# An encoder's projection stage: eight single PSUM banks, paired peaks, later key turns and another bank layout in the attention loop

## The chip, the core and the metric

The kernel runs on one core of a Trainium2 chip. The metric is device time in microseconds (us) for one launch, the median of three runs. TensorE (PE) multiplies matrices and writes PSUM, which has eight banks of 512 float32 values on each of 128 partitions. VectorE (DVE), ScalarE (ACT) and GpSimd (POOL) do the rest of the arithmetic, and SyncE (SP) issues the transfers between HBM and the on-chip memory.

## The reference

An encoder of two layers runs over 1024 tokens of width 1024, all in float32. Layer 0 mixes tokens by grouped-query attention (16 query heads, 4 key and value heads, head size 64) with normalised and rotated queries and keys; layer 1 by centred means over windows. Each layer then attends to 256 memory tokens and ends with a gated feed-forward part with a width-3 convolution. The change lies in the attention of layer 0:

```python
qkv = h @ w_qkv                      # h = rmsnorm(x, gain)
q = rmsnorm(q, q_gain); k = rmsnorm(k, k_gain)
q = apply_axial_rope(q, cos, sin) * (HEAD_DIM ** -0.5)
k = apply_axial_rope(k, cos, sin)
scores = jnp.einsum('bkgqd,bksd->bkgqs', q_blk, kt)
p = jax.nn.softmax(scores, axis=-1)
```

## The kernel before, in words

The **projection stage** is the first 165 us. Tokens are cut into eight tiles of 128 (t = 0..7). A float32 product is made of three matmuls, high by high, low by high and high by low (L755, L756, L757; `mm3`), after ACT has cut the high part of an operand (L668 for weights, L686 for x with its gain) and DVE the low part (L671, L684). One output tile of 512 columns takes eight slices of the inner size, 24 matmuls. The list `QKV` holds eight K items (keys and values of tile t, 512 columns) and sixteen Q items (two halves of eight heads by eight tiles), with "S" items, the peaks, between them.

The first four K tiles are built together, slice by slice, in the order in which x and the weights arrive: `plan_start` issues gcol (the gain), then for each k a piece of x and a piece of the weights. Before them TensorE runs `WARM` transposes of the identity (L1249).

A K or Q tile then goes through `plan_head`. ACT writes its square into PSUM (L1039), DVE sums it per head (L1043, L1044), POOL raises it to the power -1/2 (L1048, `rstd`). DVE multiplies by the rotation tables, "crossed" into a buffer `rb` (L1065) and "straight" into `kr` or `qn` (L1071); POOL adds both (L1075); DVE (L1080) or ACT (L1083) scales. Then TensorE turns the result (transposes at L1123 for keys, L1157 for queries) into PSUM, from where ACT and DVE cut high and low halves (L668, L671). `plan_k` also makes `dk`, shifted keys, which are turned too.

The row factors of x come from `plan_rows`: a load, ACT's square of a tile of x with its sum (L954, its output thrown away into a PSUM tile of two banks) and two POOL operations (L955, L956).

**Peaks.** A visit of the peaks takes 128 queries of two heads and half of the keys: one matmul over 64 rows for each head (L801) gives 512 scores per query, and their maximum (L807) is kept in `nm` for the softmax. In this stage they go to a PSUM tile of 1024 columns (pA, two banks) and one reduction of 1024 columns takes both. `PEAKS` says after which Q item one visit stands: one each after items 3 to 14.

**What sets the order.** The program text adds steps to a planner (class `Plan`). Each step has a kind with a cost, what it needs, what it gives, and which buffers it takes; "late" is a due time. The planner simulates the engines and writes the steps of each engine in the order it finds. In `main`, the product of an item is added at once and the steps behind it ("after", with the turns) `LAG` + `kind_lag` items later.

**PSUM.** In this stage the pool "psq" holds pA (two banks) and six single banks pB. In the attention loop, pool "psl", it is pO (one bank), pS (three, peaks at L801) and pT (two tiles of two banks, scores at L1311); the banks are laid out in the order in which the names are first asked for, L1256 to L1262. The loop is a planner's order as well.

## Time and profile before

| | us |
|---|---|
| median of 3 runs | 2401.65 |
| the runs | 2404.88, 2401.65, 2400.08 |
| the profiled execution's own time | 2403.06 |
| its span | 2401.30 |
| TensorE busy | 2380.1 (99%) |
| DVE, ACT, POOL busy | 1858.5, 1199.8, 407.4 |

In the rows of a timeline stand the start, the length, the engine, the line, the operation, what it writes and reads, and how often; in brackets the idle time of the engine before it and what ended it. The rows of the chain of waits (the chain of work that ended last) have start, length and what it was. In the groups by line stand total busy time and the mean of one in ns, then the idle time before. Matmuls overlap, so the distance of two starts, not the length, tells what one costs. All lines are those of the kernel before.

### The profile page before, as it was taken

The numbers are of one execution on the slowest core, as the hardware profiler recorded it, in microseconds if no ns is written. First come the engines' busy times: TensorE is split into PE (matmuls) and PEld (weight loads), VectorE is DVE, ScalarE is ACT, GpSimd is POOL, SyncE is SP. The second block draws the span as 40 slices with busy tenths as digits, with TensorE's granted clock in tenths as the row PEclk, the third lists the DMA queues.
The fourth block names the chain that finished last, engine by engine and source line by source line (L and its number), as shares of the span: only waits on it lengthen the run. The fifth ranks groups of instructions, "written<-read, shape, count | busy, mean of one in ns | idle before, by whom it ended". The sixth has DMA issues, their size and how long they took to land.

```text
span 2401.3 us, 32595 instructions
## 1 busy us (share of the span) xinstructions
PE 2380.1 (99%) x11857; PEld 1901.6 (79%) x11857; DVE 1858.5 (77%) x2594; ACT 1199.8 (50%) x1982; POOL 407.4 (17%) x394
## 2 busy tenths in 40 slices
PE   9999999999999999999999999999999999999998
PEld 7764444688988888888888888798888888888887
DVE  6669998559763898888887768986389888888875
ACT  6545556435452555555454427555255555545442
POOL 5567777310110000000000012011000000000001
PEclk9999999999999999999999999999999999999999
DMA  7000001426951243334387623695124333448752
GB/s 255 1 1 15 15 19 50 159 75 215 320 173 62 75 121 99 110 88 117 116 293 230 200 88 124 223 330 192 65 71 128 92 110 88 120 122 278 251 189 101
DMA packets 323436, 322.93 MB, mean 134 GB/s; under 512 B 32612, under 2 KB 253132, under 8 KB 323276
## 3 DMA queue, kind: packets, MB, share of 16 engines
q1 hardware_dynamic: 323276, 320.85, 41.7%
q8 instruction: 93, 1.52, 0.3%
q14 instruction: 67, 0.55, 0.1%
HBM read 233.30 MB, written 82.64 MB: 132 GB/s over the span
## 4 chain that ended last, share of the span: by engine, by line
PE 88%; DVE 4%; DMA 3%; issue 3%; ACT 1%; POOL 1%; SPq 0%; POOLq 0%; DVEq 0%; ACTq 0%
PE pB L755 22%; PE pB L757 22%; PE pB L756 22%; PE pO L1353 4%; PE pT L1311 3%; PE pA L757 3%; PE pA L755 3%; PE pA L756 3%; PE pS L801 2%; DVE R L671 1%; PE pB L324 1%; DMA scr<-in_xt 1%; PE pS L1391 1%; DMA X<-in_ffn_w_down 1%; PE pA L2367 0%
## 5 line engine op out<-in xcount | busy, mean ns | idle before, releaser
L756 PE MATMUL pB<-R,R 128*128 128x512 f32 (+1 forms) x2732 | 1030.1, 377 | 0.2 <-DVE R L671 0.2
L755 PE MATMUL pB<-R,R 128*128 128x512 f32 (+1 forms) x2668 | 1011.1, 379 | 4.2 <-DVE scr L440 2.1
L757 PE MATMUL pB<-R,R 128*128 128x512 f32 (+1 forms) x2664 | 1004.0, 377 | 1.3 <-DVE R L671 1.2
L756 PEld LDWEIGHTS pB<-R,R 128*128 128x128 f32 x2732 | 514.9, 188 | 94.0 <-DVE R L671 1.5
L755 PEld LDWEIGHTS pB<-R,R 128*128 128x128 f32 x2668 | 502.8, 188 | 101.9 <-issue 4.8
L757 PEld LDWEIGHTS pB<-R,R 128*128 128x128 f32 x2664 | 501.8, 188 | 94.5 <-DVE R L671 3.1
L668 ACT ACTIVATE R<-scr 128x512 fp32r<-128x512 f32 (+3 forms) x376 | 269.1, 745 | 230.3 <-DMA scr<-Gs 60.3
L671 DVE TENSOR_TENSOR R<-scr,R 128x512 fp32r<-128x512 f32 (+2 forms) x340 | 289.3, 878 | 35.2 <-ACT R L668 34.8
L728 POOL TENSOR_SCALAR ms<-ss 128x1 f32<-128x1 f32 x52 | 14.7, 283 | 1626.6 <-ACT R L736 1281.1
L671 DVE TENSOR_TENSOR R<-X,R 128x512 fp32r<-128x512 f32 x258 | 175.4, 687 | 49.0 <-ACT R L668 48.6
L668 ACT ACTIVATE R<-X 128x512 fp32r<-128x512 f32 x258 | 160.8, 630 | 100.1 <-PE pB L756 50.3
L438 ACT COPY scr<-pB 128x512 f32<-128x512 f32 x156 | 91.0, 583 | 177.8 <-PE pB L757 170.6
L807 DVE TENSOR_REDUCE nm<-pS 128x1 f32<-128x512 f32 x232 | 148.3, 683 | 21.2 <-PE pS L801 20.0
L1318 ACT ACTIVATE X<-pT 128x1024 f32<-128x1024 f32 x128 | 124.7, 1023 | 73.5 <-PE pT L1311 71.4
L755 PE MATMUL pA<-R,R 128*128 128x512 f32 (+1 forms) x420 | 150.6, 359 | 0.0
L757 PE MATMUL pA<-R,R 128*128 128x512 f32 (+1 forms) x420 | 150.2, 358 | 0.1
L756 PE MATMUL pA<-R,R 128*128 128x512 f32 (+1 forms) x420 | 149.9, 357 | 0.0
L1353 PE MATMUL pO<-X,XV 128*64 128x512 f32 x512 | 124.1, 605 | 0.3 <-ACT X L1318 0.3
L2058 DVE TENSOR_TENSOR X<-pB,X 128x512 f32<-128x512 f32 (+1 forms) x109 | 74.6, 685 | 61.0 <-PE pB L757 60.1
L440 DVE TENSOR_TENSOR scr<-pB,scr 128x512 f32<-128x512 f32 x156 | 107.0, 686 | 10.1 <-PE pB L757 9.9
L668 ACT ACTIVATE R<-pB 128x256 fp32r<-128x256 f32 (+1 forms) x139 | 63.1, 482 | 86.5 <-PE pB L757 43.6
L1311 PE MATMUL pT<-R,R 64*128 64x512 f32 x768 | 103.4, 392 | 0.0
(231 smaller groups left out, 2889.9 us busy)
## 6 DMA issues: line engine op xcount, KB each, us to landing
Gs<-X SPq DMA_DIRECT2D x105, 256.0 KB
X<-in_ffn_w_up SPq DMA_DIRECT2D x51, 512.0 KB
scr<-in_ffn_w_down SPq DMA_DIRECT2D x45, 512.0 KB
scr<-Gs SPq DMA_DIRECT2D x35, 512.0 KB
scr<-in_xattn_w_kv SPq DMA_DIRECT2D x32, 512.0 KB
scr<-Gs SPq DMA_DIRECT2D x42, 384.0 KB
XV<-in_ffn_w_up SPq DMA_DIRECT2D x31, 512.0 KB
Wt<-scr SPq DMA_DIRECT2D x44, 256.0 KB
```

Source lines behind the costliest of these rows:

```text
L438: self.nc.scalar.copy(out, p)
L440: self.nc.vector.tensor_tensor(out=out, in0=p, in1=out, op=OP.add)
L668: self.nc.scalar.activation(hi, src, AF.Copy)
L671: self.nc.vector.tensor_tensor(out=lo, in0=src, in1=hi.bitcast(F32), op=OP.subtract)
L755: mm(out, ah, bh, start=start, stop=False)
L756: mm(out, ah, bl, start=False, stop=False)
L757: mm(out, al, bh, start=False, stop=stop)
L807: nc.vector.tensor_reduce(NM[G][:, 2 * n + x.start:2 * n + x.stop], S, axis=AX.X, op=OP.max, negate=True)
L1311: nc.tensor.matmul(T[G, kt % 2][:, x * 512:(x + 1) * 512], left, right, start=first and (i, j) == (0, 0), stop=shifted or (not first and i ...
L1318: nc.scalar.activation(E[G, kt], T[G, kt % 2], AF.Exp)
L1353: nc.tensor.matmul(O[G][x * HD:(x + 1) * HD], V32[kt // 4][:, kt % 4, m // 4 * 2 + x], E[G, kt][:, x * 512:(x + 1) * 512], start=kt == 0, ...
L2058: nc.vector.tensor_tensor(out=x, in0=banks[b][:, c], in1=x, op=OP.add)
```

## The change

There are six edits. The pool "psq" has eight single banks (`psum("psq", 0, 8)`); a visit of the peaks takes a single bank for each of its two matmuls, and each has a reduction of 512 columns of its own. `PEAKS` puts two visits one behind the other after items 3, 5, 7, 9, 11 and 13. In `plan_rows`, ACT's square is written over the tile of x in the on-chip memory, and the two POOL operations are a step of their own. `kind_lag` puts the turns of K0 to K4 later, and some keys take a `qn` buffer for the crossed product (odd t) or for the straight one and the turn (t = 4 and 5). `plan_start` issues the weights ahead of x for each k, with gcol third, and WARM is 16. In the loop pT takes the first four banks, then pO, then pS. The lines of the kernel move by up to seven: L1123 is L1128, L1157 is L1162 and L1311 is L1318.

```diff
--- before.py
+++ after.py
@@ -38,13 +38,13 @@
 MIXER = ("D0", "D1", "D2", "D3", "D4", "D5", "D6", "M0", "D7", "M1", "O0", "M2", "M3", "O2", "T0", "M4", "M5", "M6", "O4",
          "T2", "M7", "O1", "O6", "M8", "T4", "O3", "T6", "O5", "T1", "O7")
 QS = [("Q", p, t) for p in range(2) for t in range(NT)]
-PEAKS = tuple(range(3, 15))
+PEAKS = tuple(n for n in range(3, 15, 2) for _ in range(2))
 QKV = (*(("K", t) for t in range(NT)), *(it for n, q in enumerate(QS) for it in (q, *(("S", i) for i, m in enumerate(PEAKS) if m == n))))
 LAG = 3
 QN, RB = 3, 1
 POOLED = ()
 GROUPS = [(half, m) for half in range(2) for m in range(NH // 2)]
-WARM = 20
+WARM = 16
 CHUNKS = ((0, 4 * P), (4 * P, 2 * P), (6 * P, 2 * P))
 N_SLOTS = 20
 SUMS_AT = (2, 3, 4, 5, 6)
@@ -826,12 +826,12 @@
             nc.gpsimd.tensor_scalar(out[p].rearrange("p (a b) -> p a b", b=P),
                                     self.ident[p, None, :].to_broadcast([p.stop - p.start, n, P]), 0.0, value, op0=OP.mult, op1=OP.add)
 
-        with tc.tile_pool(name="qk", bufs=1, reuse_waits="tile") as qk, self.psum("psq", 1, 6) as self.ps:
+        with tc.tile_pool(name="qk", bufs=1, reuse_waits="tile") as qk, self.psum("psq", 0, 8) as self.ps:
             sets = {0: [qk.tile([P, 2048], F32R, name="T"), *(R.get() for _ in range(3))], "K": [R.get() for _ in range(4)]}
             hT = [[R.get() for _ in range(4)] for _ in range(2)]
             tab = qk.tile([P, NT, 2, HD], F32, name="tab")
             tabs, at = {"Q": tab}, {}
-            plan = Plan(R, {}, {"scr": 6, "A": 1, "B": 6, "half": len(R.freed), "qn": QN, "rb": RB, "kr": 4, "dk": 2})
+            plan = Plan(R, {}, {"scr": 6, "B": 8, "half": len(R.freed), "qn": QN, "rb": RB, "kr": 4, "dk": 2})
             buf = lambda name, bufs, n=256: qk.tile([P, n], F32, name=name, bufs=bufs)
 
 
@@ -852,11 +852,11 @@
                     k2 = range(2 * g, 2 * g + 2)
                     x, r = (self.scr().rearrange("p (a b) -> p a b", a=2) for _ in range(2))
                     at["xT", 0, g], at["wraw", "K", g] = x, r
-                    if not g:
-                        nc.sync.dma_start(out=gcol, in_=a["gcol"])
                     for k in range(2):
+                        nc.sync.dma_start(out=r[:, k], in_=w_tile("K", g)[:, k])
                         nc.sync.dma_start(out=x[:, k], in_=x_tile(0, g)[:, k])
-                        nc.sync.dma_start(out=r[:, k], in_=w_tile("K", g)[:, k])
+                        if not g and not k:
+                            nc.sync.dma_start(out=gcol, in_=a["gcol"])
 
                 def part(lo, k, c):
                     hi, lo_ = (R.v(z, 4)[:, k % 4, c] for z in hT[0][2 * (k // 4):2 * (k // 4) + 2])
@@ -943,19 +943,22 @@
 
 
             def plan_rows(t):
-                h, junk = ("h", t), ("hjunk", t)
+                h = ("h", t)
 
                 def fetch():
                     at[h] = self.scr()
                     nc.sync.dma_start(out=at[h], in_=xin[t * P:(t + 1) * P, :])
 
                 def square():
-                    ss = self.stat(1, "ss")
-                    nc.scalar.activation(self.psA(), at[h], AF.Square, accum_out=ss)
-                    nc.gpsimd.tensor_scalar(row[:, t:t + 1], ss, HD / D, HD * EPS, op0=OP.mult, op1=OP.add)
+                    at["ss", t] = self.stat(1, "ss")
+                    nc.scalar.activation(at[h], at[h], AF.Square, accum_out=at["ss", t])
+
+                def factors():
+                    nc.gpsimd.tensor_scalar(row[:, t:t + 1], at.pop(("ss", t)), HD / D, HD * EPS, op0=OP.mult, op1=OP.add)
                     nc.gpsimd.tensor_tensor(out=first[:, t:t + 1], in0=row[:, t:t + 1], in1=self.mh[:, :1], op=OP.pow)
                 plan.add("load", 1, fetch, (), [h], [("scr", h)], late=-12.0 + 2.0 * t if t < 4 else -4.0)
-                plan.add("square", 1024, square, [h], [("first", t)], [("A", junk)], [h])
+                plan.add("grow", 1024, square, [h], [("ss", t)], uses=[h])
+                plan.add("scale", 1.8, factors, [("ss", t)], [("first", t)])
 
             def blocks(piece, x, k):
                 return self.R_(sets[piece][2 * x + k // 4]).rearrange("p (a b) -> p a b", a=4)[:, k % 4]
@@ -1033,6 +1036,8 @@
                 q3 = lambda: at[qn].rearrange("p (h c) -> p h c", h=H)
                 deferred, plain = it == QS[-1], kind == "K" or it == QS[-2]
                 eng = nc.gpsimd if deferred else nc.vector
+                cross_in = "qn" if kind == "K" and t % 2 else "rb"
+                turned_in = "kr" if kind == "K" and t not in (4, 5) else "qn"
 
                 def square():
                     at[sq] = at.pop(("v", t)) if kind == "K" else self.psB()
@@ -1058,7 +1063,7 @@
                     nc.scalar.activation(late["sq"], at[qn], AF.Square, scale=first[:, t:t + 1])
 
                 def crossed():
-                    at[rb] = buf("rb", RB, 512)[:, :H * HD]
+                    at[rb] = buf(cross_in, {"rb": RB, "qn": QN}[cross_in], 512)[:, :H * HD]
                     q5, b5 = (z.rearrange("p (h x i c) -> p h x i c", h=H, x=2, i=2) for z in (at[b], at[rb]))
                     s5 = tabs[kind][:, t, 1].rearrange("p (x i c) -> p x i c", x=2, i=2)
                     for i in range(2):
@@ -1067,7 +1072,7 @@
 
                 def straight():
                     if not deferred:
-                        at[qn] = buf("kr", 4) if kind == "K" else buf("qn", QN, 512)
+                        at[qn] = buf("kr", 4) if turned_in == "kr" else buf("qn", QN, 512)[:, :H * HD]
                     eng.tensor_tensor(out=q3(), in0=at[b].rearrange("p (h c) -> p h c", h=H),
                                             in1=tabs[kind][:, t, 0][:, None, :].to_broadcast([P, H, HD]), op=OP.mult)
 
@@ -1094,9 +1099,9 @@
                     plan.add("copy", n(100, 1), square, [b, ("first", t), ("V", t)], [sq], uses=[b])
                 else:
                     plan.add("copy", n(100, 1), square, [b, ("first", t)], [sq], [("B", sq)], [b])
-                plan.add("add", n(170, 1.25), crossed, [b, tabkey], [rb], [("rb", rb)], [b, *used])
+                plan.add("add", n(170, 1.25), crossed, [b, tabkey], [rb], [(cross_in, rb)], [b, *used])
                 plan.add("add", n(140, 1), straight, [b, tabkey, rb], [qn],
-                         [("qn" if kind == "Q" else "kr", qn)], [b, *used])
+                         [(turned_in, qn)], [b, *used])
                 plan.add("add", n(190, 1), reduce, [sq], [ss], uses=[b if kind == "K" else sq])
                 plan.add("scale", n(0.75, 0.006), rstd, [ss], [ss])
                 plan.add("scale", n(0.25, 0.0057), both, [qn, rb], [qn], uses=[qn, rb])
@@ -1184,20 +1189,22 @@
                 plan.add("load", 3, lambda: shift(0, ring[0]), ["nm", ("zero", 0)], [("zero", 0)], late=18.0)
 
             def plan_peaks(G, n):
-                b = ("s", G, n)
+                bs = [("s", G, n, x) for x in range(2)]
 
                 def emit():
-                    at[b] = self.psA()
-                    peaks(G, n, [at[b][:, x * 512:(x + 1) * 512] for x in range(2)])
+                    for b in bs:
+                        at[b] = self.psB()
+                    peaks(G, n, [at[b] for b in bs])
                 plan.add("product", 1, emit, [("KT", t, 0) for t in range(n % 2 * 4, n % 2 * 4 + 4)] + [("QT", 0, 0, n // 2)],
-                         [b], [("A", b)])
-                plan.add("tap", 1024, lambda: biggest(G, n, at.pop(b).rearrange("p (x k) -> p x k", x=2)), [b], [("nm", G, n)],
-                         uses=[b], late=3.0 if n == 7 else 9.0)
+                         bs, [("B", b) for b in bs])
+                for x, b in enumerate(bs):
+                    plan.add("tap", 512, lambda b=b, x=x: biggest(G, n, at.pop(b), slice(x, x + 1)), [b], [("nm", G, n, x)],
+                             uses=[b], late=3.0 if n == 7 else 9.0)
                 if (G, n) == (0, 7):
-                    plan.add("tiny", 1, lambda: joined(0), [("nm", 0, i) for i in range(8)], ["nm"], late=3.5)
+                    plan.add("tiny", 1, lambda: joined(0), [("nm", 0, i, x) for i in range(8) for x in range(2)], ["nm"], late=3.5)
 
             def kind_lag(it):
-                return {("K", 0): 1, ("K", 1): 1, ("K", 2): 3, ("K", 3): 3}.get(it, 0)
+                return {("K", 0): 3, ("K", 1): 3, ("K", 2): 5, ("K", 3): 5, ("K", 4): 7}.get(it, 0)
 
             def main():
                 todo, count = [], 0
@@ -1257,8 +1264,8 @@
             ones = at.tile([P, HD], F32, name="ones")
             nc.vector.memset(ones, 1.0 / HD ** 0.5)
             T, E, O, acc, ON, RS = {}, {}, {}, {}, {}, {}
-            for name, bufs in (("pO", 1), ("pS", 3)):
-                self.ps.tile([P, 512], F32, name=name, bufs=bufs)
+            for name, bufs, n in (("pT", 2, 1024), ("pO", 1, 512), ("pS", 3, 512)):
+                self.ps.tile([P, n], F32, name=name, bufs=bufs)
             plan = Plan(R, plan.over, {"A": 3, "B": 2, "O": 1, "pt": 6, "scr": 6, "qm": 3, "half": len(R.freed)})
             plan.hold("qm", ("qm", 0))
             plan.hold("scr", "late")
```

Three places show how the order moves. TensorE at the end of the product of K4 and before that of K5 (R_73 to R_76 are weights or x in high and low parts, kr the scaled keys, ident the identity), before and then with the change:

```order
L757 MATMUL pB<-R_74,R_84 128x512
L755 MATMUL pB<-R_74,R_83 128x512
L756 MATMUL pB<-R_76,R_83 128x512
L757 MATMUL pB<-R_74,R_84 128x512
L1123 MATMUL pB<-ident,kr 128x128 x4
L755 MATMUL pB<-R_73,R_81 128x512
```

```order
L757 MATMUL pB<-R_74,R_84 128x512
L755 MATMUL pB<-R_74,R_83 128x512
L756 MATMUL pB<-R_76,R_83 128x512
L757 MATMUL pB<-R_74,R_84 128x512
L755 MATMUL pB<-R_73,R_81 128x512
L756 MATMUL pB<-R_75,R_81 128x512
```

The four turns of K0 and K1 stood behind the 24 matmuls of K4; now the product of K5 follows at once, and the turns stand behind it.

TensorE between two Q items, at the first turn that has peaks behind it (qn is the scaled Q tile, R_67 the turned queries, R_73 the turned keys), before and with the change:

```order
L757 MATMUL pB<-R_70,R_84 128x512
L1157 MATMUL pB<-ident,qn 128x128 x4
L801 MATMUL pA<-R_67,R_73 128x512 x2
L755 MATMUL pB<-T,R_81 128x512
L756 MATMUL pB<-R_71,R_81 128x512
```

```order
L757 MATMUL pB<-R_70,R_84 128x512
L1162 MATMUL pB<-ident,qn 128x128 x4
L801 MATMUL pB<-R_67,R_73 128x512 x4
L755 MATMUL pB<-T,R_81 128x512
L756 MATMUL pB<-R_71,R_81 128x512
```

One visit of two matmuls stood behind each of twelve turns; two visits, four matmuls, now stand behind every second one.

TensorE where the projection ends and the loop begins, with the semaphores that an instruction waits for (the last turn, the first peaks in pS, the first scores in pT), before and with the change:

```order
L1157 MATMUL pB<-ident,qn 128x128 [waits DVE_49]
L1157 MATMUL pB<-ident,qn 128x128 x3
L801 MATMUL pS<-R_67,R_73 128x512 [waits Activation_49]
L801 MATMUL pS<-R_67,R_73 128x512 [waits DVE_49,PE_49]
L1311 MATMUL pT<-R_73,R_67 128x512 x4
L1311 MATMUL pT<-R_73,R_68 128x512 x2
```

```order
L1162 MATMUL pB<-ident,qn 128x128 [waits DVE_49]
L1162 MATMUL pB<-ident,qn 128x128 x3
L801 MATMUL pS<-R_67,R_73 128x512 x2
L1318 MATMUL pT<-R_73,R_67 128x512 [waits PE_49]
L1318 MATMUL pT<-R_73,R_67 128x512 x3
L1318 MATMUL pT<-R_73,R_68 128x512 x2
```

The first two peaks waited for ACT and for DVE; with the change they wait for neither. From here on the order of every engine is the same in both kernels.

## The prediction, made before the changed kernel had run

> **What bounds the kernel now.** I read the page first, then the busy time by stretches, then what TensorE waits for, and last the timelines of the places that these name. The page's first part and its chain that ended last:
>
> ```profile
> PE 2380.1 (99%) x11857; PEld 1901.6 (79%) x11857; DVE 1858.5 (77%) x2594; ACT 1199.8 (50%) x1982; POOL 407.4 (17%) x394
> PE 88%; DVE 4%; DMA 3%; issue 3%; ACT 1%; POOL 1%; SPq 0%; POOLq 0%; DVEq 0%; ACTq 0%
> ```
>
> TensorE (PE) is busy for 2380.1 of 2401.3 us, so 21 us is all that the removal of waits could give in the whole program; anything more must come from TensorE doing less or doing it faster. The change edits the projection, which is the first 165 us. Busy time by stretches of the span (time, length, then each engine's busy time; PEclk is the granted clock):
>
> ```profile
> 30.00:40.00 10.00, 8.07 (x32) 6.38 (x31) 7.18 (x25) 9.94 (x24) 8.12 (x13) 0.86 0.51 176
> ...
> 80.00:120.00 40.00, 40.00 (x183) 30.86 (x183) 25.39 (x49) 21.45 (x70) 21.68 (x17) 1.00 0.00 1
> ...
> 160.00:170.00 10.00, 7.94 (x56) 5.04 (x57) 8.47 (x16) 5.14 (x9) 7.95 (x6) 1.00 0.01 2
> 170.00:260.00 90.00, 89.66 (x544) 44.20 (x542) 81.49 (x112) 49.48 (x62) 70.05 (x36) 1.00 0.09 13
> ```
>
> Two stretches have idle TensorE, 30 to 40 and 160 to 170, about 2 us each; and in the first of them the clock is granted only in part. Between and after them TensorE runs through, so time saved ahead of 170 should reach the end undiminished. The waits of TensorE in the first 240 us (total, times, longest) name the same two places:
>
> ```profile
> PE pB L1123 <- ACT R L686: 1.9, 1, 1.9
> PE pS L801 <- DVE R L671: 1.5, 1, 1.5
> PE pS L801 <- DVE nm L807: 0.9, 2, 0.6
> ```
>
> All sums below are made against the profiled execution, 2403.06 us with a span of 2401.30. The shown runs have a median of 2401.65 and reach from 2400.08 to 2404.88, so the profiled one is 1.4 above the median and inside their spread.
>
> **The key turns (kind_lag).** The turns of K0 and K1 stand behind the fourth new K product and wait for the scaled keys. PE and, last, DVE, around the wait; the rows between are from the chain of waits (start, length to the next step):
>
> ```profile
> 33.62 0.38 PE L1123 MATMUL pB<-ident,kr 128*128 128x128 f32 x2
> 35.94 0.41 PE L1123 MATMUL pB<-ident,kr 128*128 128x128 f32 x2 [1.93 <-ACT R L686]
> ...
> 37.67 0.43 PE pB L757
> ...
> 40.23 0.43 PE pB L757
> 40.65 0.27 PE pB L755
> 40.92 0.23 PE pB L756
> ...
> 35.36 0.43 DVE L1080 TENSOR_TENSOR kr<-kr,rs 128x256 f32<-128x256 f32 x1 [1.93 <-POOL kr L1075]
> ```
>
> The wait is put down to ACT, but DVE's scaling at 35.36 ends at 35.79, just before the turn, and itself waited 1.93 us for POOL; POOL's chain is the cause. The change puts one more product of 24 matmuls, 24 x 0.23 = 5.5 us (0.23 from the row at 40.92), ahead of this turn. TensorE then reaches it at about 33.62 + 5.5 = 39.1, some 3 us after the keys are ready, if the key chain is as fast as now. So the wait goes: the turn at 35.94 would have followed the one at 33.62 by 0.22, so about 2.1 us. Then, from the row at 37.67 to that at 40.23, each matmul takes 0.43 where it takes 0.23 behind them. That is seven matmuls at 0.2 more and about 0.2 at the two edges, 1.6 to 1.7 us. This is the stretch of the granted clock 0.86. I take it as a consequence of the idle time before it. **B: -2.1 - 1.7 = -3.8**, and -2.1 if the clock stretch stays. The other turns move as well; the row says 1.9 us for a turn that comes too early, so a new wait of that kind is bounded by 0 and +1.9; each gains 5.5 us of distance and loses only the place of a chain that others now share. I take 0.
>
> The Trainium skill, page "TensorE: Matmul & The Clock Gate", Part 1, says that the clock falls to half after an idle window of about 3.4 us. Here an idle time of 1.93 us stands before a stretch of half clock, so trace and page differ on how much idle time it takes. By the page's rule the 1.7 us would not be the stall's doing and B would be -2.1; that is a rival below.
>
> **The peaks in pairs.** Peak products (L801) use 64 rows of the array, the rest 128. Turns on the chain of waits, without a peak pair (73.59 to 79.56) and with one (79.56 to 86.16), then PE's timeline and, last, twelve 64-row matmuls of the loop in a row:
>
> ```profile
> 73.59 0.44 PE pB L1157 x4
> 79.56 0.44 PE pB L1157 x4
> ...
> 86.16 0.44 PE pB L1157 x4
> ...
> 79.93 0.50 PE L801 MATMUL pA<-R,R 64*128 64x512 f32 x2
> 80.36 0.50 PE L755 MATMUL pB<-T,R 128*128 128x512 f32 x1
> 80.70 0.39 PE L756 MATMUL pB<-R,R 128*128 128x512 f32 x1
> ...
> 165.24 1.39 PE pT L1311 x12
> ```
>
> A block without peaks takes 5.97 us, one with them 6.60: a pair of peak matmuls costs 0.63. Inside a run, 64-row matmuls cost 1.39/12 = 0.116 each, so 0.23 a pair; the other 0.40 lies at the change of shape (0.43 from the pair to L755, 0.34 to the next). The change makes twelve visits of one pair into six of two, so six changes of shape are saved: **C: -6 x 0.40 = -2.4**. A wait inside a pair of visits would split it again; its bounds are 0 and -2.4 for lost gain. The peaks now take single banks of PSUM which others also use. The banks a visit takes were last used by the visit two blocks earlier, read by DVE then, or by the turn one block earlier, 6 us before; I take no split.
>
> Two reductions of 512 replace one of 1024:
>
> ```profile
> L807 DVE TENSOR_REDUCE nm<-pS 128x1 f32<-128x512 f32 x92 | 58.8, 684 | 9.7 <-PE pS L801 9.3
> L807 DVE TENSOR_REDUCE nm<-pA 128x2 f32<-128x1024 f32 x12 | 14.6, 1216 | 2.4 <-PE pA L801 2.4
> ```
>
> That is 2 x 0.684 - 1.216 = 0.15 us more for each of 12 on DVE, 1.8 us in all. DVE is busy for 25.39 of 40 us among these blocks and has room for it; if it had none, the price would be at most +1.8.
>
> **The border to the loop.** PE, then DVE:
>
> ```profile
> 161.61 0.46 PE L801 MATMUL pS<-R,R 64*128 64x512 f32 x1 [1.49 <-DVE R L671]
> ...
> 164.75 0.50 PE L801 MATMUL pS<-R,R 64*128 64x512 f32 x1 [0.57 <-DVE nm L807]
> 164.75 1.88 PE L1311 MATMUL pT<-R,R 64*128 64x512 f32 x12
> ...
> 156.99 0.69 DVE L1080 TENSOR_TENSOR qn<-qn,rs 128x512 f32<-128x512 f32 x1 [1.11 <-POOL qn L1075]
> ...
> 160.05 1.42 DVE L671 TENSOR_TENSOR R<-pB,R 128x256 fp32r<-128x256 f32 x4 [1.23 <-ACT R L668]
> ...
> 164.00 2.49 DVE L807 TENSOR_REDUCE nm<-pS 128x1 f32<-128x512 f32 x4 [1.19 <-PE pS L801]
> ```
>
> Before, the second pS stands in a bank that DVE's L671 reads until 161.47. In the new layout the first two pS and the first pT take banks that nobody holds. They can run at 159.6 to 161.0, and the second pT needs a bank that L671 has left at 160.8. Then four more pS come; they wait one by one for DVE's reductions (2.49/4 = 0.62 each), which can start at 161.5 rather than in pieces. The second run of pT could start at about 163.4 instead of 164.75: -1.3. Against it, the scaled Q block that the last turn needs (156.99 + 0.69 = 157.7, used at 159.1) now comes up to 0.1 late by my count, since its square stands behind its two multiplications. **D: -1.2**, bounds 0 and -1.5. The cover of the loop's own DVE work behind it, 81.49 of 90 us, is thin: a rival.
>
> **The start.** ACT, DVE, PE; then the chain of waits with SP's queue (issues) and the transfer:
>
> ```profile
> 4.73 0.63 ACT L668 ACTIVATE R<-scr 128x512 fp32r<-128x512 f32 x1 [2.52 <-DMA scr<-in_attn_w_qkv]
> ...
> 7.07 0.72 ACT L686 ACTIVATE R<-scr,gcol 128x512 fp32r<-128x512 f32 x1 [0.91 <-DMA scr<-in_xt]
> 7.74 0.63 ACT L668 ACTIVATE R<-scr 128x512 fp32r<-128x512 f32 x1
> ...
> 8.49 0.68 DVE L671 TENSOR_TENSOR R<-scr,R 128x512 fp32r<-128x512 f32 x1
> ...
> 5.82 0.79 PE L755 MATMUL pB<-R,R 128*128 128x512 f32 x1
> ...
> 8.97 0.39 PE L755 MATMUL pB<-R,R 128*128 128x512 f32 x1
> ...
> 0.72 0.39 SPq L856
> ...
> 1.63 0.43 SPq L859
> 2.10 4.94 DMA scr<-in_xt
> ```
>
> The first weights are issued at 0.72 instead of 1.63 (L859), the first x stays second, and gcol (L856) moves to third. ACT's first copy at 4.73 moves by up to 0.9 with the weights, and the first matmul from 5.82 to about 4.9. But for the second k, ACT still takes x first (7.07) and weights second (7.74), and x is now the one that lands last. x in the slot of the former weights lands at about 7.7, so ACT's pair ends at 7.7 + 0.72 + 0.63 = 9.1 where it ended at 7.74 + 0.63 = 8.4, and DVE's weight half ends 0.67 later. The first matmul of that k (8.97) moves little, its third by up to 0.7. From there TensorE ran through before. **A: +0.3**, between -0.9 (transfers no longer bind) and +0.7. The four warm-up transposes that are dropped lie ahead of the first matmul and cost nothing.
>
> The squares written in place, the two POOL operations behind an own due time, and the crossed keys in the qn buffers stay off TensorE's path by these rows: 0, with +1.9 as the bound for a turn made late. **Sum: +0.3 - 3.8 - 2.4 - 1.2 = -7.1**; 2396.0 from the profiled execution, 2394.6 from the median. I take the middle, **2395.3**.
>
> **The rivals.** First, the clock stretch stays although the stall goes (the skill's rule, or it is there in this execution alone): 2395.3 + 1.7 = 2397.0. For it speaks that the border's 1.49 us of idle time was followed by no such stretch; against it that the stretch begins 1.3 us behind the longest idle time of the stage. Second, the pairs of peaks are split by a bank still being read, so the change does not do what it says: +2.4, 2397.7. Third, the gain of the border is given back, since DVE, 81.49 of 90 us, sets the pace of the loop and has no earlier start of its reductions: +1.2, 2396.5; against it stands TensorE's 89.66 of 90. Fourth, a start worse than mine: the twelve matmuls of the first k, 4.9 + 12 x 0.23 = 7.7, end 1.4 us before the second k's operands at 9.1, and half clock follows that idle time: +0.4 above my term and 1.7, 2397.4. Fifth, the slower side: the six visits wait for the previous visit's four reductions, because these now hold four of only eight banks and their due time lets DVE do them late. With 4 x 0.684 = 2.7 us per visit that is 6 x 2.7 = +16.4, 2411.7. It decides for slower from (2406.45 - 2395.3)/6 = 1.9 us per visit. For it: the banks are now shared by all; against it: DVE is busy for 25.39 of 40 us there, and the previous visit lies two blocks, over 12 us, back.
>
> **How the numbers follow.** A measurement of this kernel can tell 0.2% from no change, 4.8 us: faster is below 2396.85, slower above 2406.45. The forecast has 0.50, its own range 2393.5 to 2397.0; the rivals in order 0.14, 0.12, 0.09, 0.08, 0.07. Below 2396.85 lie nine tenths of the first, near half of the first and third rivals, and a quarter of the second and fourth: 0.45 + 0.06 + 0.03 + 0.05 + 0.02 = 0.61. Slower 0.07, the rest 0.32. The range 2391.5 to 2400.0 takes in all bounds of the terms but the slow rival, and below the terms' ends with the median as the base.
>
> **What would show it.** No wait of the key turns and no granted clock under 1 between 30 and 50 (B). Blocks of Q that alternate between 5.97 and about 6.83 us, with four peaks in one visit (C). No wait of pS for L671 near 159, and the second run of pT 4.8 instead of 6.1 us behind the start of the last turns (D). The first matmul near 4.9, its second k with a gap before it (A). Wrong: any wait of TensorE for L807 or L671 between 80 and 155, a new wait at the turns of K2 to K5, or a loop that starts earlier and ends at the same time.

## The result and the profile after

| | before | with the change |
|---|---|---|
| median of 22 runs each (us) | 2402.55 | 2397.78 |
| the runs | 2399.79 to 2405.54 | 2395.46 to 2400.73 |
| ratio, 95% interval | | 0.998, 0.9974 to 0.9986 |
| the profiled execution's own time | 2403.06 | 2396.91 |
| its span | 2401.3 | 2394.8 |

The change gives 4.77 us. The interval of the ratio lies below 1, so a gain is shown; it falls just short of the 0.2% (4.8 us) that the prediction asked for to call the kernel faster. Forecast were 7.1 us; between the two profiled executions there are 6.15, since the one before lies 0.5 above its median and the one after 0.9 below its own. The page after, first part and the chain that ended last:

```profile
PE 2376.7 (99%) x11853; PEld 1899.4 (79%) x11853; DVE 1861.5 (78%) x2606; ACT 1200.3 (50%) x1982; POOL 404.7 (17%) x394
PE 90%; DVE 4%; issue 3%; DMA 2%; POOL 1%; ACT 0%; SPq 0%; POOLq 0%; DVEq 0%; ACTq 0%
```

TensorE is busy 3.4 us less (2380.1 before) in a span that is 6.5 us shorter, so about half of the difference is idle time and half is work that costs TensorE less. Busy time by stretches after (time, length, the engines in the order PE, PEld, DVE, ACT, POOL, then the granted clock, DMA share and GB/s):

```profile
30.00:40.00 10.00, 10.00 (x48) 8.32 (x47) 8.44 (x25) 9.97 (x25) 6.63 (x10) 1.00 0.71 237
40.00:50.00 10.00, 10.00 (x50) 8.28 (x49) 8.57 (x20) 6.83 (x15) 9.37 (x12) 1.00 0.58 203
50.00:60.00 10.00, 9.10 (x46) 7.22 (x45) 6.91 (x17) 1.98 (x6) 8.88 (x11) 1.00 0.29 103
...
160.00:170.00 10.00, 9.66 (x59) 4.90 (x57) 9.72 (x15) 4.90 (x6) 9.48 (x5) 1.00 0.07 2
```

Both stretches with idle TensorE are nearly closed: 30 to 40 has TensorE busy throughout at full clock (8.07 at 0.86 before), and 160 to 170 has 9.66 (7.94 before; the border itself now lies at 154 to 159, and 150 to 160 has 9.78). But a new one has come, 50 to 60, with 0.9 us idle. The waits of TensorE in the first 240 us name it (total, times, longest):

```profile
PE pB L1128 <- POOL dk L1122: 0.9, 1, 0.9
```

TensorE's timeline after, at the places of the four terms. First the turns of K0 and K1, then those of K4 and K5 ahead of the first Q product, then the border to the loop:

```profile
39.25 0.39 PE L757 MATMUL pB<-R,R 128*128 128x512 f32 x1
39.48 0.60 PE L1128 MATMUL pB<-ident,kr 128*128 128x128 f32 x4
...
51.79 0.38 PE L1128 MATMUL pB<-ident,qn 128*128 128x128 f32 x2
53.03 0.44 PE L1128 MATMUL pB<-ident,dk 128*128 128x128 f32 x2 [0.87 <-POOL dk L1122]
...
53.91 0.48 PE L755 MATMUL pB<-T,R 128*128 128x512 f32 x1
...
154.33 1.19 PE L1162 MATMUL pB<-ident,qn 128*128 128x128 f32 x8
155.45 0.50 PE L801 MATMUL pS<-R,R 64*128 64x512 f32 x2
...
158.99 1.65 PE L1318 MATMUL pT<-R,R 64*128 64x512 f32 x11
```

The turns of K0 and K1 wait for nothing any more. The eight turns of K4 and K5 take 2.12 us (51.79 to 53.91) where eight in a row take 0.79 (45.42 to 46.21 in the same trace): 1.33 us are lost there. From the last turns to the second run of pT there are 4.66 us (6.08 before).

The Q blocks on the chain of waits (start, length, what):

```profile
71.57 0.44 PE pB L1162 x4
...
77.54 0.44 PE pB L1162 x4
77.98 0.66 PE pB L801 x4
...
84.35 0.44 PE pB L1162 x4
```

A block without peaks takes 5.97 us and one with two visits 6.81; before, each block with one visit took 6.60.

Put together by stretches of TensorE, each from the start of one matmul to that of another, in the two profiled executions (us):

| stretch | before | after | difference | forecast |
|---|---|---|---|---|
| to the first matmul of K4 | 28.18 | 28.60 | +0.42 | +0.3 |
| from there to the first Q product | 27.72 | 25.31 | -2.41 | -3.8 |
| from the first Q product to the last turns | 102.77 | 100.42 | -2.35 | -2.4 |
| last turns to the second run of pT | 6.08 | 4.66 | -1.42 | -1.2 |
| all of it | 164.75 | 158.99 | -5.76 | -7.1 |

Three of the four terms came out within 0.22 us. The second did not, and it holds the wait above.

### The profile page after: what moved, and what is told of

It reads as the page before. It is cut to its first block, busy times and chain, and to the rows that moved or that the text cites. A ratio compares the mean times of both kernels' runs of the same rounds, so it can differ in the third digit from the quotient of the medians.

```text
span 2394.8 us, 32603 instructions
## 1 busy us (share of the span) xinstructions
PE 2376.7 (99%) x11853; PEld 1899.4 (79%) x11853; DVE 1861.5 (78%) x2606; ACT 1200.3 (50%) x1982; POOL 404.7 (17%) x394
## 4 chain that ended last, share of the span: by engine, by line
PE 90%; DVE 4%; issue 3%; DMA 2%; POOL 1%; ACT 0%; SPq 0%; POOLq 0%; DVEq 0%; ACTq 0%
PE pB L755 23%; PE pB L757 23%; PE pB L756 22%; PE pO L1360 4%; PE pT L1318 3%; PE pA L757 3%; PE pA L755 3%; PE pA L756 3%; PE pS L801 2%; DVE R L671 1%; PE pB L324 1%; DMA scr<-in_xt 1%; PE pS L1398 1%; PE pA L2374 0%; POOL scr L1374 0%
## 5 line engine op out<-in xcount | busy, mean ns | idle before, releaser
L668 ACT ACTIVATE R<-scr 128x512 fp32r<-128x512 f32 (+3 forms) x376 | 269.1, 744 | 228.3 <-DMA scr<-Gs 59.9
L671 DVE TENSOR_TENSOR R<-scr,R 128x512 fp32r<-128x512 f32 (+2 forms) x340 | 288.6, 877 | 27.5 <-ACT R L668 27.3
L671 DVE TENSOR_TENSOR R<-X,R 128x512 fp32r<-128x512 f32 x258 | 175.1, 686 | 48.8 <-ACT R L668 48.4
L668 ACT ACTIVATE R<-X 128x512 fp32r<-128x512 f32 x258 | 160.9, 630 | 98.7 <-PE pB L756 50.3
L668 ACT ACTIVATE R<-pB 128x256 fp32r<-128x256 f32 (+1 forms) x139 | 62.9, 483 | 83.0 <-PE pB L757 43.7
L1318 PE MATMUL pT<-R,R 64*128 64x512 f32 x768 | 103.0, 392 | 0.0
```

What stands on the lines that cost most here:

```text
L668: self.nc.scalar.activation(hi, src, AF.Copy)
L671: self.nc.vector.tensor_tensor(out=lo, in0=src, in1=hi.bitcast(F32), op=OP.subtract)
L1318: nc.tensor.matmul(T[G, kt % 2][:, x * 512:(x + 1) * 512], left, right, start=first and (i, j) == (0, 0), stop=shifted or (not first and i ...
```

## The experiments

Every kernel is timed against the kernel before on its own chip. K4 to K7 are the keys' products, Q0 and Q1 the first two products of queries; the border is the way from the last turns of the projection to the loop's second run of pT. Half clock means a granted clock of 0.5: the starts of matmuls of 512 columns then lie 0.43 us apart instead of 0.23. Where only one time is given, a few us of it are chance, and the verdict rests on the trace. The table has the start of TensorE's milestones in us: the first matmul, the first of K4, the first Q product, the second, the last turns, the second run of pT.

| kernel | first | K4 | Q0 | Q1 | last turns | pT | us |
|---|---|---|---|---|---|---|---|
| before | 5.82 | 28.18 | 55.90 | 61.86 | 158.67 | 164.75 | 2403.06 |
| before_again | 5.99 | 28.29 | 56.81 | 62.78 | 159.62 | 166.47 | 2403.41 |
| changed kernel | 5.38 | 28.60 | 53.91 | 59.86 | 154.33 | 158.99 | 2396.91 |
| changed_again | 5.01 | 28.57 | 53.24 | 59.19 | 153.65 | 158.32 | 2394.8 |
| old_key_turns | 5.66 | 29.71 | 54.86 | 60.81 | 155.30 | 159.96 | 2394.94 |
| single_visits | 5.68 | 29.32 | 53.59 | 59.54 | 156.38 | 162.48 | 2398.87 |
| old_start | 5.79 | 29.58 | 53.51 | 59.45 | 153.94 | 158.60 | 2394.36 |
| old_layout | 5.02 | 28.24 | 54.84 | 62.37 | 156.81 | 162.86 | 2397.83 |
| warm_20 | 6.61 | 29.05 | 53.40 | 59.36 | 153.79 | 158.46 | 2394.16 |
| dk_first | 5.53 | 28.37 | 53.62 | 59.60 | 154.07 | 158.73 | 2396.0 |
| dk_first_old_start | 5.82 | 28.31 | 53.55 | 59.52 | 154.02 | 158.68 | 2395.2 |
| dk_first_old_start_again | 5.82 | 27.97 | 53.86 | 59.82 | 154.29 | 158.95 | 2395.22 |
| bank_freed_early | 5.91 | 28.17 | 52.13 | 59.47 | 153.94 | 160.02 | 2397.93 |
| differences_on_dve | 6.06 | 28.42 | 56.99 | 62.96 | 157.40 | 162.78 | 2399.86 |

The times in the last column are those of the profiled executions.

### The kernel before, once more

> The kernel before, unchanged, profiled a second time. Theory (the half-clock stretch follows the stall): PE again waits 1.9 to 2.1 us at the turns of K0 and K1, and behind it matmul starts lie 0.43 us apart for about 3.4 us, as long as most of the idle time falls into one window of the clock; the product of K5 then ends near 43.1. Rival (the stretch comes by chance): the same wait, no stretch, and K5 ends near 41.4.

The kernel is unchanged; the question was what of its trace belongs to the one execution. TensorE's timeline at the turns of K0 and K1, then at the border:

```profile
36.86 0.41 PE L1123 MATMUL pB<-ident,kr 128*128 128x128 f32 x2 [2.74 <-ACT R L686]
...
37.96 0.63 PE L755 MATMUL pB<-R,R 128*128 128x512 f32 x1
...
40.52 0.63 PE L755 MATMUL pB<-R,R 128*128 128x512 f32 x1
...
162.56 0.47 PE L801 MATMUL pS<-R,R 64*128 64x512 f32 x1 [1.48 <-DVE R L671]
...
166.47 0.79 PE L1311 MATMUL pT<-R,R 64*128 64x512 f32 x1
```

The stall and the half clock behind it (starts 0.43 apart from 37.96 to 40.95) are there again, so they belong to the kernel; the stall is 2.74 us, longer than the 1.9 to 2.1 expected. The stall of the border is the same 1.48 us, but this time half clock followed it as well (the stretch 160 to 170 has a granted clock of 0.83, where the first trace has 1.00), and the way to the second run of pT took 6.85 us instead of 6.08.

### Undo the later key turns

```diff
-                return {("K", 0): 3, ("K", 1): 3, ("K", 2): 5, ("K", 3): 5, ("K", 4): 7}.get(it, 0)
+                return {("K", 0): 1, ("K", 1): 1, ("K", 2): 3, ("K", 3): 3}.get(it, 0)
```

> The changed kernel with the old turn lags of K0 to K4 (1, 1, 3, 3, 0); everything else as changed. If the later turns give what the trace says: the stall at the turn of K0 and K1 is back, 2.1 us (and 1.7 more if half clock follows), and the new wait of the changed kernel for POOL's key differences before the first Q product is gone. The first Q product then starts at 54.6 (no stretch) to 56.3 (with it) instead of 53.91. Rival (the new wait before Q has nothing to do with the lags): the wait of about 1 us near 52 stays.

```profile
35.85 0.77 PE L1128 MATMUL pB<-ident,kr 128*128 128x128 f32 x4 [0.54 <-DVE kr L1085]
```

The stall came back at 0.54 us only, where 2.1 were expected, with no half clock behind it; the trace has no wait for dk ahead of Q0, which starts at 54.86. The keys were no earlier: the turn runs at 35.85, that of K1 before at 35.94. TensorE was later: in this execution its clock was half until 10.09 (below), K4 began at 29.71 instead of 28.18, and these 1.53 us are about what the wait lost (1.93 to 0.54). So the worth of later turns depends on when TensorE arrives. Against the kernel with the new turns and the same late start (old_start, K4 at 29.58) it is 1.35 us at Q0. This kernel is no clean undo, then: two things differ from the changed kernel's trace, the turns and the late start. That all of the 3.8 can reach Q0 is seen further on, in bank_freed_early: from the first matmul of K4 to Q0 it takes 23.96 us, against 27.72 before.

### Undo the pairs

```diff
-PEAKS = tuple(n for n in range(3, 15, 2) for _ in range(2))
+PEAKS = tuple(range(3, 15))
```

> The changed kernel with one visit of the peaks after each of the items 3 to 14, in single banks. If a change of shape costs 0.40 us: twelve blocks of 6.60 instead of six of 6.82 among six of 5.97, so the last turns start 2.4 us later, at 156.7 instead of 154.33. Rival (the eight single banks already gave the gain by themselves): they start within 0.5 us of 154.33.

From Q1 to the last turns TensorE takes 96.84 us, against 94.47 in the changed kernel and 96.81 before. The pairs are worth 2.37 us, and the single banks with two reductions alone nothing. What was not expected is at the border, where the new layout stands unchanged in this kernel:

```profile
159.32 0.47 PE L801 MATMUL pS<-R,R 64*128 64x512 f32 x1 [1.48 <-DVE R L671]
```

The wait of the kernel before is back, and the second run of pT comes 6.10 us behind the last turns. The likely reason is that the eight banks are handed out in turn: with the visits in other places the last turns sit in other banks, and the second peaks again meet one that DVE still reads. The trace does not name the banks, so that they are the reason is argued and not shown.

### Undo the order of the first transfers; then only the warm-up

```diff
+                    if not g:
+                        nc.sync.dma_start(out=gcol, in_=a["gcol"])
                     for k in range(2):
-                        nc.sync.dma_start(out=r[:, k], in_=w_tile("K", g)[:, k])
                         nc.sync.dma_start(out=x[:, k], in_=x_tile(0, g)[:, k])
-                        if not g and not k:
-                            nc.sync.dma_start(out=gcol, in_=a["gcol"])
+                        nc.sync.dma_start(out=r[:, k], in_=w_tile("K", g)[:, k])
```

> The changed kernel with the old order of the first transfers (gcol, then x ahead of the weights), still 16 warm-up transposes. If ACT's order (x, then weights) makes the new order late: the first matmul comes later, near 5.8, the first matmul by the second weights at 8.97 and the next at 9.23 instead of 9.65, and the product of K4 ends 0.4 us earlier, near 33.4 for its last matmul's start instead of 33.81. Rival (the later full clock at the start, 7.2 instead of 6.5, did it, because four warm-up transposes are missing): full clock is late again and the product ends at 33.8 or later.

```diff
-WARM = 16
+WARM = 20
```

> The changed kernel with 20 warm-up transposes instead of 16. If the idle time ahead of the first matmul (0.4 to 0.8 us in the four runs with 16) kept the clock at half: no idle time there, full clock from 7.2 us at the latest, and the 97th matmul (the first of K4) starts at 28.6 or before, where three runs with 16 had 29.3 to 29.7. Rival (where the window falls alone decides): half clock until 9 or 10 us again. On the end: if POOL's key differences set the start of the first Q product, it stays at 53.5 to 53.9 all the same; if TensorE does, it comes at 52.6.

TensorE's first matmuls with the old order of transfers and 16 warm-up transposes (old_start):

```profile
3.74 1.27 PE L1256 MATMUL pB<-ident 128*128 128x128 f32 x5
5.79 0.80 PE L755 MATMUL pB<-R,R 128*128 128x512 f32 x1 [0.77 <-ACT R L686]
...
9.80 0.41 PE L755 MATMUL pB<-R,R 128*128 128x512 f32 x1
```

The same with 20 transposes (dk_first_old_start, whose start is that of the kernel before):

```profile
3.75 2.12 PE L1256 MATMUL pB<-ident 128*128 128x128 f32 x9
5.82 0.80 PE L755 MATMUL pB<-R,R 128*128 128x512 f32 x1
...
7.21 0.39 PE L755 MATMUL pB<-R,R 128*128 128x512 f32 x1
```

In old_start the clock is half until 9.80, in dk_first_old_start until about 7. The executions differ: of the six with 16 transposes, three run at half clock until 9.3 to 10.1 (old_key_turns, single_visits, old_start), and three reach full clock by 7.4, both traces of the changed kernel and old_layout. Of the eight with 20, all reach it by 7.2. The three late ones are those with 0.64 to 0.77 us of idle time ahead of the first matmul; the other three with 16 have 0.36 at most. So the missing transposes can cost 1 us or more at K4, but not in every execution. The order of the transfers shows no such effect: with 20 transposes the new order (dk_first) begins K4 at 28.37 and the old one at 28.31 and 27.97. In warm_20 the transfers of the new order landed late (first matmul at 6.61 after a wait of 0.88), so K4 began at 29.05 and not by 28.6 as expected; still no matmul ran at half clock. But none of this reaches Q0: in the table old_start, warm_20, single_visits and both traces of the changed kernel begin K4 between 28.57 and 29.58 and Q0 between 53.24 and 53.91, in no order that follows K4.

### Undo the bank layout

```diff
-            for name, bufs, n in (("pT", 2, 1024), ("pO", 1, 512), ("pS", 3, 512)):
+            for name, bufs, n in (("pO", 1, 512), ("pS", 3, 512)):
```

> The changed kernel with the old layout of the loop's banks (pO and pS first, then pT). If the layout gives the gain at the border: pS waits for DVE's L671 again, and from the start of the last turns to the second run of pT it takes 6.1 us instead of 4.66, +1.4. Rival (the pairs give it, since single visits lost it with the new layout): 4.7 us.

```profile
53.97 0.44 PE L1128 MATMUL pB<-ident,dk 128*128 128x128 f32 x2 [2.15 <-POOL dk L1122]
...
55.23 0.63 PE L756 MATMUL pB<-R,R 128*128 128x512 f32 x1
...
159.75 0.97 PE L1318 MATMUL pT<-R,R 64*128 64x512 f32 x6 [1.30 <-DVE R L671]
```

At the border 1.39 us come back (6.05 from the last turns to the second run of pT, against 4.66): the layout gives the border's gain. The wait itself is at pT and not at pS, as was expected. The surprise is again ahead of Q0, in a part that this edit doesn't touch. The same wait for dk is 2.15 us here, and half clock followed it: starts 0.43 apart from 55.23 to 58.22, Q1 at 62.37 instead of 59.86. ACT and POOL show what stands ahead of it (both of old_layout):

```profile
43.89 1.06 ACT L668 ACTIVATE R<-scr 128x1024 fp32r<-128x1024 f32 x1 [2.58 <-DMA scr<-in_attn_w_qkv]
...
46.16 0.44 ACT L1044 ACTIVATE pB<-pB,first 128x256 f32<-128x256 f32 x1
```

```profile
50.35 0.43 POOL L957 TENSOR_SCALAR row<-ss 128x1 f32<-128x1 f32 x1
50.86 1.42 POOL L958 TENSOR_TENSOR first<-row,mh 128x1 f32<-128x1 f32 x1
52.37 0.74 POOL L919 TENSOR_SCALAR gq<-gq 128x64 f32<-128x64 f32 x1
53.19 1.41 POOL L1122 TENSOR_TENSOR dk<-qn,kr 128x256 f32<-128x256 f32 x2
```

ACT cuts a piece of the Q weights (L668) that has not landed, and the square of K5 (L1044), on which the keys' chain hangs, stands behind it in ACT's order. The same copy waited 0.23 us in the changed kernel's trace, and its square ran at 44.50 instead of 46.16. On POOL the row factors of the last tile and gq stand ahead of the two differences and take 2.8 us (50.35 to 53.19). So two things add up, a late transfer and POOL's order. The transfer alone doesn't make the wait, as the next trace shows.

### The changed kernel, once more

> The changed kernel, unchanged, profiled a second time and timed beside the next. If the wait before the first Q product belongs to the change and not to one execution: PE waits 0.3 to 2.2 us for POOL's differences or DVE's L671 again, and the first Q product starts at 53.5 to 54.9 whatever the start did; median near 2397.8. Rival (that wait was one execution's): it starts 24 us behind the first matmul of K4.

Median 2396.61 of 11 runs (2394.28 to 2398.27) against 2402.11; ratio 0.9977 (0.9968 to 0.9986). In its trace the copy waits 1.67 us for the weights and TensorE only 0.2 for dk. In the first trace the copy waited less (0.23) and TensorE longer (0.87): there POOL's power of K4 took 1.99 us (44.46, shown in the last section) where here it takes 1.01, and the differences came at 52.25 where here they come at 51.57. TensorE's first product of Q starts at 53.24 (53.91 in the first trace, 56.81 and 55.90 in the two of before). So the gain up to Q0 is 2.0 to 3.6 us, by which pair of executions one takes, and the new wait is a matter of the execution: 0.2, 0.9 and (in old_layout) 2.2 us in kernels with the same work up to there. Both expectations are narrowly missed: the wait is under 0.3 and Q0 before 53.5, yet Q0 comes 24.67 us behind the first matmul of K4 and not 24.

### The differences ahead of the row factors on POOL

Two edits, with 20 warm-up transposes again: gq and the last tile's row factors need the difference of K5, so that POOL makes the differences first; and the same with the old order of the first transfers.

```diff
-                    plan.add("scale", 0.5, scaled, ["gQ", ("kr", 5)], ["gQ"])
+                    plan.add("scale", 0.5, scaled, ["gQ", ("dk", 5)], ["gQ"])
...
-                plan.add("scale", 1.8, factors, [("ss", t)], [("first", t)])
+                plan.add("scale", 1.8, factors, [("ss", t)] + [("dk", 5)] * (t == 7), [("first", t)])
```

> As warm_20, and on POOL the differences of K4 and K5 ahead of the last tile's row factors and of the query gain. If POOL's order made the wait before the first Q product: no wait of the turns of K4 and K5, and the first Q product starts 24.0 us behind the first matmul of K4 (28.6 + 24.0 = 52.6) instead of 25.3. Rival (the chain ahead of the differences, squares and powers of K5, is late itself): it starts at 53.3 or later.

> As dk_first with the old order of the first transfers: the changes that the traces show as gains, without those that they show as losses. If the terms add: the first matmul of K4 at 28.2 and the first Q product at 52.2, 1.7 us ahead of the changed kernel's, 2396.1 against its 2397.8 and 2402.5 before, ratio 0.9973. Rival (what is gained ahead of the loop is given back in it, as 1.1 us of the change's was): 2397.2 or more.

The wait for dk is gone in both traces, and another of the same size stands behind it. TensorE, then DVE, of dk_first:

```profile
52.21 0.44 PE L1128 MATMUL pB<-ident,dk 128*128 128x128 f32 x2
53.62 0.50 PE L755 MATMUL pB<-T,R 128*128 128x512 f32 x1 [0.98 <-DVE R L671]
...
50.35 2.88 DVE L995 TENSOR_TENSOR R<-scr,R 128x1024 fp32r<-128x1024 f32 x2
53.15 0.41 DVE L671 TENSOR_TENSOR R<-pB,R 128x256 fp32r<-128x256 f32 x1
```

The first Q product takes the bank of a turned key, which DVE reads (L671) only after two cuts of Q weights (L995). Q0 starts at 53.62 and 53.55, as in the kernels that wait for dk, and not at 52.6 and 52.2 as expected. dk_first_old_start has a median of 2394.84 of 7 runs, ratio 0.9969 (0.9958 to 0.9981). That is below the 2396.1 expected, but since Q0 didn't come early, this speaks for none of the terms. It was run once more, unchanged:

> dk_first_old_start again, beside the first of this call. If its 2394.84 was right: 2394.8 to 2395.8, ratio near 0.997. Rival (seven runs were too few, and it is no better than the changed kernel): 2396.6 or more.

This time the median is 2395.97 of 8 runs, ratio 0.9978 (0.9967 to 0.9988), with Q0 at 53.86 and Q1 at 59.82; a wait of 0.47 us for K5's difference is back in this trace, ahead of 0.97 for L671. The changed kernel has 0.998 and 0.9977, so no gain over it is shown.

### That bank freed early as well

To dk_first_old_start comes a due time for DVE's low half of the first keys, so that it goes ahead of the weights.

```diff
-                        self.low(steps_of(t) if wide else keys(0, t), keys(1, t), at.pop(bank)[:, wide])
+                        self.low(steps_of(t) if wide else keys(0, t), keys(1, t), at[bank][:, wide])
...
-                    plan.add("add", 330, partial(put, 1), [bank, ("KT", t, 1 if wide else 0)], [("KT", t, 2)], uses=[bank])
+                    plan.add("add", 330, partial(put, 1), [bank, ("KT", t, 1 if wide else 0)], [("KT", t, 2)], uses=[bank],
+                             late=4.0 if t < 2 else None)
```

> As dk_first_old_start, and the low parts of the turned K0 and K1 on DVE ahead of the low parts of the Q weights, so that the bank of the first Q product is free. If DVE's L671 is the last link: no wait of the first Q product, which starts at 52.3 instead of 53.55, and the time is 1.2 us under that kernel's 2394.84, 2393.6. Rival (a further link, the first Q weights or their low parts, stands behind it): 53.2 or later, 2394.5 or more.

Q0 starts at 52.13, 0.79 after its turns begin, so nothing waits there. The next turn does:

```profile
58.41 0.44 PE L1128 MATMUL pB<-ident,kr 128*128 128x128 f32 x2 [0.50 <-DVE kr L1085]
59.27 0.44 PE L1128 MATMUL pB<-ident,dk 128*128 128x128 f32 x2 [0.43 <-POOL dk L1122]
```

and Q1 starts at 59.47, as everywhere. At the border 1.4 us are lost (6.08): the second peaks wait 1.33 us for L671, as in single_visits. Median 2397.09 of 11 runs, ratio 0.9979 (0.997 to 0.9988).

### The differences on DVE

To these edits comes the difference of keys on DVE instead of POOL, and the layout pT, pS, pO.

```diff
-                    nc.gpsimd.tensor_tensor(out=at[dk], in0=at[kr[t]], in1=at[kr[t - 2]], op=OP.subtract)
+                    nc.vector.tensor_tensor(out=at[dk], in0=at[kr[t]], in1=at[kr[t - 2]], op=OP.subtract)
...
-                    plan.add("scale", 2.4, differ, [("kr", t), ("kr", t - 2)], [dk], [("dk", dk)], [kr[t], kr[t - 2]])
+                    plan.add("add", 256, differ, [("kr", t), ("kr", t - 2)], [dk], [("dk", dk)], [kr[t], kr[t - 2]], late=9.0 if t in (4, 5) else None)
```

> As dk_first_old_start, with all key differences on DVE instead of POOL, DVE's low parts of the turned K0 and K1 early, and pS ahead of pO in the loop's layout (so that the first peaks of the loop still need no bank of DVE's). If POOL's row of work between 34 and 60 us sets the start of the second Q product, which came at 59.2 to 59.8 in every kernel with the later turns whatever was mended before it: the first Q product starts at 52.2 and the second at 58.2, and the time is about 1 us under that of dk_first_old_start. Rival (DVE, which takes the work over, sets it): the second Q product starts at 59.2 or later, and the time is the same or longer.

```profile
48.83 0.54 PE L1128 MATMUL pB<-ident,dk 128*128 128x128 f32 x2 [2.66 <-DVE dk L1122]
...
49.60 0.63 PE L756 MATMUL pB<-R,R 128*128 128x512 f32 x1
```

DVE made the difference of K4 ahead of that of K3, with a cut of Q weights between, and the turn of K3 waited 2.66 us; half clock followed (granted clock 0.95 in the stretch 40 to 50 and 0.88 in 50 to 60). Median 2401.08 of 11 runs, ratio 0.9994 (0.9985 to 1.0003): all of the gain is gone. It was meant to show whether POOL alone sets Q1 at 59.5; it missed that, and the question stays open.

## Why the prediction was right or wrong

**The key turns (forecast -3.8, measured -2.4 in the profiled pair).** What the part says of the stall held: no wait of the turns of K0 and K1 (39.48), whose keys were ready 2.6 us before (DVE's scaling ends at 36.87), and no half clock between 30 and 50. The products of K4 and K5 with the turns of K0 and K1 take 15.10 us before (28.18 to 43.28) and 11.23 after (28.60 to 39.83), 3.87 less. The step that failed is "a new wait of that kind is bounded by 0 and +1.9; each gains 5.5 us of distance and loses only the place of a chain that others now share. I take 0". K5's turn gained no distance. Its lag is unchanged, and the steps of `main` wait in one list in order (its counter grows by two for each item), so it stays behind K7's product, which ends 3.8 us earlier: the turns there began at 51.79 instead of 55.55. K4's turn gained one product, but its difference lost its place on POOL. POOL before, then DVE and POOL after:

```profile
45.71 0.74 POOL L1117 TENSOR_TENSOR dk<-kr 128x256 f32<-128x256 f32 x1 [0.60 <-DVE kr L1080]
```

```profile
47.18 0.43 DVE L1085 TENSOR_TENSOR qn<-qn,rs 128x256 f32<-128x256 f32 x1 [0.68 <-POOL qn L1080]
...
49.42 0.42 POOL L957 TENSOR_SCALAR row<-ss 128x1 f32<-128x1 f32 x1
...
52.25 1.41 POOL L1122 TENSOR_TENSOR dk<-qn,kr 128x256 f32<-128x256 f32 x2
```

K4's difference was made at 45.71 before. After, its operand is scaled at 47.61, but POOL makes it at 52.25, behind K5's chain, the row factors and gq, and K5's difference follows it. So the first thing that TensorE waits for there is K4's difference, and it is late by POOL's order. The wait is 0.9 us idle and 1.33 us in all, 0.69 in the second trace, inside the bounds; in old_layout, with the same work up to there, 2.15 us idle lie above the bound of 1.9. Behind it stand further links: the transfer of Q weights, ACT's order, DVE's sums, DVE's low halves. Taking away one link (dk_first), then a second (bank_freed_early), only brought the next to light. In the kernels with later turns and no other mishap, Q1 starts between 59.2 and 59.9, for starts of K4 from 28.0 to 29.6. In most of them the preparation of the keys sets the pace ahead of Q0 or Q1. In old_start nothing waits there, and TensorE itself, late at K4 (29.58), sets it; that it ends at the same place is chance. Before the change TensorE set the pace there too (Q1 at 61.9). What holds Q1 near 59.5 in all the others is not settled.

**The clock as a consequence of the idle time** was right for this stall: it went with it, so the first rival (the stretch stays) falls. After every other stall of 2 us or more half clock followed too (old_layout 2.15, differences_on_dve 2.66); after those of 0.2 to 1.0 us none did. Between lies the border's 1.48, followed by it in one execution and not in two others; stalls of 1.30 (old_layout) and 1.33 (bank_freed_early) were not followed by it. The Trainium skill, page "TensorE: Matmul & The Clock Gate", Part 1, puts the fall behind an idle window of about 3.4 us that runs freely. That the stretches here last about 3.4 us (37.58 to 40.95 in before_again, 54.84 to 58.22 in old_layout) and that the same stall is punished or not agrees with free-running windows; the size of the idle time doesn't: 1.5 to 2.7 us were enough.

**The pairs (-2.4; measured -2.35 on the profiled pair, 2.37 by undoing them)** held in size and in mechanism: blocks of 5.97 and 6.81 us (forecast 5.97 and 6.83), four peaks in one visit, no wait between 80 and 155. The second rival (split visits) and the fifth (a visit waits for the reductions of the previous one) fall. Each reduction takes what the rows of before say, 680 ns against 684:

```profile
L807 DVE TENSOR_REDUCE nm<-pB 128x1 f32<-128x512 f32 x24 | 15.2, 680 | 0.0
```

Together they keep DVE busy for 15.2 us, 0.6 more than before (14.6) and not 1.8, since 24 of 680 ns make 16.3 and some of them overlap.

**The border (-1.2; measured -1.42)** held, with more behind it than the prediction saw. It named the layout alone; the runs show that the gain needs the layout (old_layout loses it) and that the layout is not enough (single_visits and bank_freed_early lose it with the new one). What else it needs, probably the place at which the hand-out of eight banks stands when the stage ends, is not shown. The third rival, that the loop gives it back, is not confirmed: from the first matmul into pO to the last there are 266.18 and 265.59 us in the two traces of before, 266.90 and 265.72 in those after. That is the spread between executions, and no difference can be told.

**The start (+0.3; measured +0.42).** The sum was right, and one reason wrong. "The four warm-up transposes that are dropped lie ahead of the first matmul and cost nothing" failed: in three of six executions without them the clock stays at half for 3.6 to 4.4 us behind the first matmul, and K4 begins up to 1.5 us later than before. In the two traces of the changed kernel it does not, so the +0.42 measured has other parts: half clock until 7.25 instead of 6.41, and a gap at the second k. The fourth rival saw half clock at the start, but from a gap at the second k; the gap was 0.3 us (9.14 to 9.65, where starts are 0.23 apart) and no half clock followed it. And the term doesn't reach the end: with the later turns starts of K4 from 28.57 to 29.58 end in much the same Q0.

**The total.** The forecast was 2395.3, the measurement 2397.78, inside the range (2391.5 to 2400.0), 0.8 above the forecast's own. The gain of the medians, 4.77, is 2.3 short of the 7.1. At the turns of K4 and K5, 1.4 of them are found in the profiled pair. The rest lies between executions, since that pair gained 6.15 where the medians gained 4.77. Of the changed kernel's executions one trace meets the wait for dk at 0.2 us and one at 0.9; old_layout, with the same work up to there, at 2.15 with half clock behind it. How often each happens is not shown by so few traces.

## What to carry to other kernels

When a stall is removed, ask what the faster engine catches up with: go to its next waits, one by one, and see by how much each operand is early. The operand with the least margin, here the differences of K4 and K5 behind other work in POOL's order, caps the gain. A turn that is put later can lose what it gains when the engine that prepares it puts its work later too. Look for what fills an engine ahead of its first work before calling it free, and read a layout of buffers together with the hand-out of the buffers before it.

## What the runs showed of the hardware

**Half clock after short stalls.** An idle time of 1.48 us before the loop was followed by half clock in one of three executions, idle times of 1.30 and 1.33 us in neither of two, idle times of 1.93, 2.15, 2.66 and 2.74 us each time. It lasts about 3.4 us and costs 0.2 us per matmul of 512 columns, by that 1.6 to 1.7 us on top of the stall where TensorE sets the pace; at the border of before_again, where waits follow, the way took 0.77 us longer.

**POOL beside DVE.** POOL's power on 128x4 takes about 1.0 us alone and twice that beside a DVE cut of 1024 columns with two operands in the on-chip memory. The changed kernel's POOL and DVE:

```profile
44.46 1.99 POOL L1053 TENSOR_TENSOR rs<-ss,mh 128x4 f32<-128x4 f32 x1
47.11 1.02 POOL L1053 TENSOR_TENSOR rs<-ss,mh 128x4 f32<-128x4 f32 x1
```

```profile
44.33 1.25 DVE L995 TENSOR_TENSOR R<-scr,T 128x1024 fp32r<-128x1024 f32 x1
47.52 1.22 DVE L995 TENSOR_TENSOR R<-scr,T 128x1024 fp32r<-128x1024 f32 x1
```

The first power starts just behind the cut and ends 0.87 us after it (45.58 to 46.45), the second started before its cut and wasn't slowed. The Trainium skill, page "SBUF — State Buffer", section "SBUF: two separate sides", has a DVE operation with two inputs in SBUF and a GpSimd operation that reads SBUF take a shared pair of ports as a lock for the whole instruction; who starts first keeps it, and the other waits. The slowed power agrees with that. The second cut doesn't: it started at 47.52, while the power ran (47.11 to 48.13), and took 1.22 us all the same.
